# Eight gate projections moved ahead of the attention as four pairs of quarter products, and the softmax multiply moved from VectorE to GpSimd

## The chip, the cores and the metric

The kernel runs on one core of one Trainium2 chip. Five engines of that core run side by side, each in the order of its own instructions: TensorE (PE, with its weight loads PEld), VectorE (DVE), ScalarE (ACT), GpSimd (POOL) and SyncE (SP), which here issues nearly all DMAs. The metric is device time in microseconds, the median of several runs. A trace of one execution is there beside it.

## What is computed

One step of an encoder layer for 1,024 prompt tokens and 64 sample tokens (T = 1,088), model width 1,024. A normalised input is projected to 6,144 columns. Two attention branches of eight heads by 64 follow, and two gates of 1,024 columns each:

```python
h = rms_norm(x, norm_w) @ w_in                       # (1088, 1024) @ (1024, 6144)
sb_q, sb_k, sb_v, sb_z, cb_q, cb_k, cb_v, cb_z, g_sb, g_cb = jnp.split(h, SPLIT_POINTS, axis=-1)
...
# branch A, stick-breaking: beta = sigmoid(q.k/8), w[t,s] = beta[t,s] * prod_{s<j<t} (1 - beta[t,j])
# branch B, band attention: softmax(q.k/8 + rel_bias) over a band of at most 9 chunks of 64 keys
...
b_sb = (o_sb * silu(z_sb)) @ w_proj_sb
b_cb = (o_cb * silu(z_cb)) @ w_proj_cb
h = sigmoid(g_sb) * b_sb + sigmoid(g_cb) * b_cb
y = x + h @ w_out
```

New keys and values are outputs too. Everything is float32; the projections are made of three products each of a high and a low part in a reduced format (high by high, high by low, low by high).

## The kernel before

The order of every engine's instructions is the order of the program (`manual_schedule`, line 38). The stages are:

1. **Natural products** (line 464): eight blocks of 256 columns of the projection, tokens on the partitions.
2. **Pairs** (lines 606 to 657): eight *pairs* of 128-column blocks, listed in `pairs` (lines 145 to 149). A pair is a 2 by 2 product of halves (two halves of the 1,024 inputs, two blocks of columns, two halves of the tokens), made from seven quarter products and sums of them instead of eight. Each quarter product has 24 matmuls: two stretches of tokens `XC` (256 and 288), four blocks of 128 inputs, three parts. `prep` and `presum` make the weights of a quarter product (ACT, POOL, and DVE for the sums) five products ahead; `emit` (line 565) evicts a finished quarter. For a `silu` pair it takes a Sigmoid on ACT and a multiply on DVE, and for a kind `sig`, which is in the code but in no pair before, the Sigmoid alone; the result goes to DRAM.
3. **Attention** (lines 1169 to 1202): 144 steps `seq`, 72 of the stick-breaking branch `sb` and then 72 of the band branch `cb`. A step is one block of query tokens of one head. For each of four head pairs p the blocks come in the order t = 8 (the 64 sample tokens, 576 keys), 0, 1, ... 7, two heads each. In a step with `sb` there are n = 128 (t + 1) keys, with `cb` at most 640.
4. **Merge and output**: projections of the branches (lines 873 and 917) and the last product (line 1404).

In one turn i of the attention's loop the program issues, in this order: `qk(i)`, the scores; half of the turn's filling; `av`, the product with the values, if one is due; `tr(i - 3)`, the transposes of the finished weights of three steps before; `mid(i)`; the other half of the filling.

`qk` multiplies into a buffer `z` of PSUM (three buffers; a step of more than 512 keys takes two). For `sb`, ACT then takes two Sigmoids, into `kp` and `be`. For `cb`, DVE adds the bias and finds the extreme (line 1030), and ACT takes Exp with the sum of the row (line 1034). `mid` is on DVE: for `sb` a scan (line 1044) and a multiply (line 1045), for `cb` the reciprocal of the sum (line 1047) and the multiply of the row by it (line 1048). `tr` transposes on PE into one of two buffers `pt`, and ACT or DVE in turn copies them to `wT` (lines 1085 and 1087). `av` multiplies `wT` by the values, and DVE multiplies the result by the gate `zt` (line 1118). `be` has four buffers, `wT` four.

**The filling.** `run_fill` (line 766) is a generator that gives one matmul at a time: first the `units` (lines 150 and 151), 128 columns of the projection each, 72 matmuls over all tokens in chunks `CH` of 384, 384 and 320, and then the projection of branch `sb`, `proj_sb`, 288 matmuls. Before the change there are 16 units: eight Sigmoid gates of `sb` and eight raw gates of `cb`. The weights of the next unit are split in the second chunk of each unit: the high part on ACT (line 115), the low part on POOL (line 122). Two units (six times `fill(24)`, line 1157) run ahead of step 0; the steps get as many matmuls as lines 1161 to 1188 share out, in proportion to n for `sb` and to n + 150 for `cb`; what is left runs after the loop. Before the last unit the generator stops until the flag `late["sb"]` is set (lines 982 and 1190), in the sixth step of `cb`: what a turn asks for until then is kept in `owed` and asked for at once afterwards.

The attention's inputs come by DMAs that `prefetch` (line 1123) issues on SP. `load_bias` (line 1146) loads a head's bias and has POOL put two masks into it (lines 1150 and 1151), which wait for the load.

Of the kernel before, what the change touches and what calls it, by code (L numbers as in the profile page):

```python
# [10 lines left out]
AF = mybir.ActivationFunctionType  # L11
OP = mybir.AluOpType
# [5 lines left out]
KT = 8  # L18
# [14 lines left out]
def hybrid_step_kernel(ctx: ExitStack, tc: tile.TileContext, x_prompt, x_sample, c_sbk, c_sbv, c_cbk, c_cbv,  # L33
# [3 lines left out]
    V, A, G, TE, SP = nc.vector, nc.scalar, nc.gpsimd, nc.tensor, nc.sync  # L37
# [15 lines left out]
    def rows(t):  # L53
        return 128 if t < 8 else NS
# [26 lines left out]
    d_g = {b: [dram.tile([128, T], F32, name=f"d_g{b}{u}") for u in range(KT)] for b in ("sb", "cb")}  # L81
# [63 lines left out]
    pairs = []  # L145
    for p in (0, 2):
        pairs += [("k", 512 + 128 * p, p), ("q", 128 * p, p)]
    for p in (0, 2):
        pairs += [("silu", 1536 + 128 * p, d_z["sb"][p:p + 2]), ("silu", 3584 + 128 * p, d_z["cb"][p:p + 2])]
    units = [("ev_act", 4096 + 128 * j, (AF.Sigmoid, d_g["sb"][j])) for j in range(KT)]  # L150
    units += [("ev_act", 5120 + 128 * j, (AF.Copy, d_g["cb"][j])) for j in range(KT)]

    def put_t(dst, src):
        A.activation(dst[0], src, AF.Copy)
# [43 lines left out]
    with ExitStack() as ph:  # L198
# [251 lines left out]
        for i in range(nb):  # L450
            for ti, t in enumerate(TO):
                r = rows(t)
# [91 lines left out]
    with ExitStack() as ph:  # L544
# [70 lines left out]
        for i in range(len(pairs)):  # L615
            bank, s1, u2, u3 = {}, {}, {}, {}
            for s in range(7):
                n = 7 * i + s
# [375 lines left out]
    def band(b, t):  # L994
        if t == 8:
            return 0, 576
        if b == "sb":
            return 0, (t + 1) * 128
        k0 = max(0, t - 4)
        return k0, (t + 1 - k0) * 128  # L1000
# [36 lines left out]
    def mid(i):  # L1037
        b, p, t, hd = seq[i]
        r = rows(t)
        k0, n = band(b, t)  # L1040
        be, kp = st[i]
        if b == "sb":
            im = imp[0:64, 960 - n:960] if t == 8 else imp[:, NP - n:NP]
            V.tensor_tensor_scan(kp[:r, n - 1::-1], kp[:r, n - 1::-1], im[:, ::-1], 0.0, op0=OP.mult, op1=OP.add)  # L1044
            V.tensor_tensor(out=be[:r, :n], in0=be[:r, :n], in1=kp[:r, 1:n + 1], op=OP.mult)  # L1045
        else:
            V.reciprocal(kp[:r, 3:4], kp[:r, 2:3])
            V.tensor_scalar(be[:r, :n], be[:r, :n], kp[:r, 3:4], None, op0=OP.mult)

    def wbase(b, j):  # L1050
        return max(0, 2 * j - 4) if b == "cb" and j < 4 else 0
# [106 lines left out]
        flush()  # L1158
        f()
    FP = 180  # L1160
    n_sb = 72 * 7
    n_cb = 72 * (len(units) - 9) + FP
    wt = {"sb": lambda n: n, "cb": lambda n: n + 150}
    tot = {b: sum(wt[b](band(b, t)[1]) for bb, p, t, hd in seq if bb == b) for b in ("sb", "cb")}
    amount = {"sb": n_sb, "cb": n_cb}
# [3 lines left out]
    for i in range(len(seq) + LAG + 1):  # L1169
        m = 0  # L1170
        if i < len(seq):
            b, p, t, hd = seq[i]
# [22 lines left out]
        if 0 <= i - LAG < len(seq):  # L1195
            tr(i - LAG)
            b, p, t, hd = seq[i - LAG]
            if hd == 1 and (t % 2 == 1 or t == 8):
                avq.append((b, p, t // 2 if t < 8 else 4))
        if i < len(seq):  # L1200
            mid(i)
# [175 lines left out]
    for i in range(2):  # L1377
# [3 lines left out]
        for q, s in enumerate(OP_):  # L1381
            n = 8 * i + q
# [13 lines left out]
            for c in range(2) if s != "b" else ():  # L1396
# [9 lines left out]
                p = ps[:]  # L1406
# [17 lines left out]
                if s in (3, 4, 5, 6):  # L1424
# [4 lines left out]
                    if s == 4:  # L1429
                        p, x = u3[c], xrs.pop((i, 1, 1, c))  # L1430
                    V.tensor_tensor(out=y, in0=p, in1=x, op=OP.add)
                    store_y(i, w, half, c, y)
            for s_, wh, wl in ([] if n == 0 else [(0,) + first, (3, wh, wl)] if n == 1 else
                               [(s, wh, wl)] if s in (0, 3, "b", 5) else []):
                w = 0 if s_ in (0, 3) else 1
                r = 0 if s_ in (0, "b") else 1
# [55 lines left out]
```

## Time and profile before

| | |
|---|---|
| median of 3 runs | 1012.59 us (1009.52 to 1013.1) |
| the profiled execution's own time | 1008.24 us |
| its span, first to last instruction | 1006.3 us |
| TensorE's mean granted clock in it | 0.997 |
| busy: PE, DVE, ACT, POOL | 97%, 65%, 47%, 32% |

The profile's page sums each engine's busy time, the chain of work that ended last, and groups of instructions (line, engine, operation, tiles, shape, count, busy time, mean duration, idle time ahead of them and what ended it). Views of the trace cut this by a window of time, by line, by tile, or give the instructions in order. Matmuls overlap in their pipeline, so that the duration of one is longer than the time from one to the next; what a matmul costs is read from a run of them. In the profiled execution the pairs begin at 226.2 us, the first unit at 403.4, the first step of `cb` waits for its bias until 630.9, and the last steps of the attention end at about 855 us.

### The profile page before, as it was taken

Reading aid. Unit: us, or ns where it says so; the run is one execution under the profiler, and the core shown is the slowest. Engines: PE = TensorE matmul, PEld = TensorE weight load, DVE = VectorE, ACT = ScalarE, POOL = GpSimd, SP = SyncE. Lnnn points to the kernel's source line nnn. Section 1 sums busy time; section 2 is a strip of 40 time slices with the busy share of each in tenths; the row PEclk is TensorE's granted clock in tenths of the full one; section 3 lists DMA queues with packets and bytes.
Section 4 is the critical chain, followed back from the end, with each engine's and each line's share of the span. In section 5 each row is a group of like instructions: output and inputs, shape, how many; then the busy total and the mean of one; then the engine's idle time right before and its main releaser. Section 6 shows DMA issues by size and latency. Waiting matters only on the chain.

```text
span 1006.3 us, 20170 instructions
## 1 busy us (share of the span) xinstructions
PE 978.0 (97%) x7512; PEld 929.9 (92%) x7512; DVE 655.2 (65%) x1233; ACT 473.1 (47%) x1075; POOL 322.0 (32%) x338
## 2 busy tenths in 40 slices
PE   5999999999999999999999999999999899989998
PEld 5999999999889999988898878898989798989998
DVE  5466673894354554189798878465766766399735
ACT  5544443444343433277666656454445543366220
POOL 3276663205343543211111101110202200387452
PEclk9999999999999999999999999999999999999999
DMA  6736577434555332697565644775756954863632
GB/s 227 231 105 211 184 247 275 129 100 155 173 163 165 119 98 77 173 244 192 137 169 149 160 116 119 206 201 152 192 151 184 266 168 130 250 213 100 194 128 95
DMA packets 180865, 169.83 MB, mean 169 GB/s; under 512 B 34912, under 2 KB 167136, under 8 KB 180640
## 3 DMA queue, kind: packets, MB, share of 16 engines
q1 hardware_dynamic: 172048, 160.23, 53.7%
q10 hardware_dynamic: 8720, 8.33, 2.6%
q8 instruction: 59, 0.97, 0.4%
q14 instruction: 38, 0.31, 0.1%
HBM read 109.78 MB, written 58.72 MB: 167 GB/s over the span
## 4 chain that ended last, share of the span: by engine, by line
PE 86%; DMA 4%; DVE 3%; ACT 3%; issue 2%; SPq 1%; POOL 1%; DVEq 0%; ACTq 0%
PE acc L464 19%; PE acc L773 17%; PE b L634 15%; PE b L1404 8%; PE o L1115 7%; PE pt L1076 6%; PE b L917 4%; PE z L1025 3%; PE z L1024 3%; PE acc L873 3%; DMA d_ksbT<-hl 1%; PE pk L349 1%; DMA wrawx<-in_w_in_dram 1%; PE pt L277 1%; DVE be L1045 1%
## 5 line engine op out<-in xcount | busy, mean ns | idle before, releaser
L122 POOL TENSOR_TENSOR wlo<-wraw,whi 128x1024 fp32r<-128x1024 f32 x30 | 74.2, 2472 | 245.0 <-ACT whi L115 211.4
L773 PE MATMUL acc<-xm,whi 128*128 128x384 f32 (+1 forms) x384 | 128.6, 335 | 0.0
L1044 DVE TENSOR_TENSOR_SCAN kp<-kp,imp 64x576 f32<-64x576 f32 (+8 forms) x72 | 102.8, 1428 | 21.2 <-ACT kp L1027 21.0
L1034 ACT ACTIVATE be<-be,sm 128x640 f32<-128x640 f32 (+5 forms) x72 | 50.8, 705 | 97.0 <-DVE sm L1030 97.0
L1076 PE MATMUL pt<-ident,be 128*128 128x128 f32 (+2 forms) x608 | 89.5, 271 | 6.2 <-DVE wT L1087 3.4
L1085 ACT ACTIVATE wT<-pt 128x512 f32<-128x512 f32 (+3 forms) x130 | 63.5, 502 | 55.3 <-PE pt L1076 55.3
L1076 PEld LDWEIGHTS pt<-ident,be 128*128 128x128 f32 (+2 forms) x608 | 68.1, 139 | 18.1 <-issue 6.4
L464 PE MATMUL acc<-whi,xa 128*128 128x256 f32 x256 | 74.2, 292 | 0.0
L773 PEld LDWEIGHTS acc<-xm,whi 128*128 128x128 f32 x384 | 72.5, 189 | 1.1
L464 PE MATMUL acc<-wlox,xm 128*128 128x256 f32 x256 | 70.8, 278 | 0.0
L464 PE MATMUL acc<-whi,xm 128*128 128x256 f32 x256 | 70.7, 278 | 0.0
L464 PE MATMUL acc<-wlo,xa 128*128 128x256 f32 x256 | 70.7, 278 | 0.0
L464 PE MATMUL acc<-whix,xb 128*128 128x256 f32 x256 | 70.6, 278 | 0.0
L464 PE MATMUL acc<-whix,xm 128*128 128x256 f32 x256 | 70.6, 278 | 0.0
L1115 PE MATMUL o<-wT,vp 128*64 128x256 f32 (+1 forms) x608 | 67.2, 361 | 0.1
L1045 DVE TENSOR_TENSOR be<-be,kp 64x576 f32<-64x576 f32 (+8 forms) x72 | 60.3, 837 | 10.3 <-DVE kp L1044 0.5
L1027 ACT ACTIVATE kp<-z 128x384 f32<-128x384 f32 (+6 forms) x112 | 54.3, 484 | 24.3 <-PE z L1025 22.9
L773 PE MATMUL acc<-xa,wlo 128*128 128x384 f32 (+1 forms) x192 | 65.4, 341 | 0.0
L773 PE MATMUL acc<-xa,whi 128*128 128x384 f32 (+1 forms) x192 | 65.4, 341 | 0.0
L773 PE MATMUL acc<-xm,wlo 128*128 128x384 f32 (+1 forms) x192 | 65.1, 339 | 0.0
L1115 PEld LDWEIGHTS o<-wT,vp 128*64 128x64 f32 x608 | 43.1, 138 | 23.7 <-issue 8.2
L773 PE MATMUL acc<-xb,whi 128*128 128x384 f32 (+1 forms) x192 | 64.1, 334 | 0.0
(298 smaller groups left out, 3012.6 us busy)
## 6 DMA issues: line engine op xcount, KB each, us to landing
wraw<-in_w_in_dram SPq DMA_DIRECT2D x35, 512.0 KB, 4.5
wrawx<-in_w_in_dram SPq DMA_DIRECT2D x13, 512.0 KB, 4.4
sq<-d_qsbT SPq DMA_DIRECT2D x32, 192.0 KB, 4.8
sq<-d_qcbT SPq DMA_DIRECT2D x32, 192.0 KB, 3.7
gt<-d_gsb SPq DMA_DIRECT2D x30, 192.0 KB, 2.7
xt<-in_x_prompt_dram SPq DMA_DIRECT2D x8, 512.0 KB, 5.7
d_kcbT<-hl SPq DMA_DIRECT2D x8, 512.0 KB, 4.6
d_qcbT<-hl SPq DMA_DIRECT2D x8, 512.0 KB, 5.7
```

Of the source, the lines that this page charges most:

```text
L122: (eng or G).tensor_tensor(out=l, in0=raw, in1=h[:].bitcast(F32), op=OP.subtract)
L464: TE.matmul(ps, x, w, start=m == 0, stop=m == len(steps) - 1)
L634: TE.matmul(ps[:, :m], w[:, hl_, k], right[s](x)[:, k, a:b], start=s < 3 and k == 0 and e == 0, stop=k == 3 and e == 2, skip_group_check=s ...
L773: TE.matmul(ps[:, :b - a], w[:, k], xk(x, k)[:, a:b], start=k == 0 and n == 0, stop=k == KT - 1 and n == 2)
L1027: A.activation(kp[:r, x:y], z[:r, :m], AF.Sigmoid, scale=-0.125)
L1034: A.activation(be[:r, :n], be[:r, :n], AF.Exp, bias=kp[:r, j:j + 1], scale=-1.0, accum_out=kp[:r, 2:3])
L1044: V.tensor_tensor_scan(kp[:r, n - 1::-1], kp[:r, n - 1::-1], im[:, ::-1], 0.0, op0=OP.mult, op1=OP.add)
L1045: V.tensor_tensor(out=be[:r, :n], in0=be[:r, :n], in1=kp[:r, 1:n + 1], op=OP.mult)
L1076: TE.transpose(pt[:kr, x, :r], be[:r, kb * 128:kb * 128 + kr], ident[:r, :r])
L1085: A.activation(w[:, sl:sl + m, q0:q0 + r], pt[:, :m, :r], AF.Copy)
L1115: TE.matmul(o[hd * 64:hd * 64 + 64, c0:c1], vv[:kr, kb, hd * 64:hd * 64 + 64], wT[b, p, j, hd, s // 4][:kr, s % 4, c0:c1], start=si == 0, ...
L1404: TE.matmul(ps[:, t], left[s](xs_, k)[:, ts_], wt_[:, k], start=s < 3 and t == k == e == 0, stop=k == 3 and e == 2, skip_group_check=s > 2 ...
```

## The change

The eight Sigmoid gates of `sb` leave the units and become four pairs of kind `sig` at the end of the list. Eight units, the raw gates of `cb`, stay as filling. The sharing of the filling follows: `sb` gets 360 matmuls of it in place of 504, `cb` 252 in place of 684. The first two units still run ahead of step 0. And in the band attention the multiply by the reciprocal goes from DVE to POOL; the reciprocal stays on DVE.

```diff
@@ -147,8 +147,8 @@
     for p in (0, 2):
         pairs += [("silu", 1536 + 128 * p, d_z["sb"][p:p + 2]), ("silu", 3584 + 128 * p, d_z["cb"][p:p + 2])]
-    units = [("ev_act", 4096 + 128 * j, (AF.Sigmoid, d_g["sb"][j])) for j in range(KT)]
-    units += [("ev_act", 5120 + 128 * j, (AF.Copy, d_g["cb"][j])) for j in range(KT)]
+    pairs += [("sig", 4096 + 128 * p, d_g["sb"][p:p + 2]) for p in range(0, KT, 2)]
+    units = [("ev_act", 5120 + 128 * j, (AF.Copy, d_g["cb"][j])) for j in range(KT)]
 
@@ -1045,7 +1045,7 @@
         else:
             V.reciprocal(kp[:r, 3:4], kp[:r, 2:3])
-            V.tensor_scalar(be[:r, :n], be[:r, :n], kp[:r, 3:4], None, op0=OP.mult)
+            G.tensor_scalar(be[:r, :n], be[:r, :n], kp[:r, 3:4], None, op0=OP.mult)
 
@@ -1158,8 +1158,8 @@
     FP = 180
-    n_sb = 72 * 7
-    n_cb = 72 * (len(units) - 9) + FP
+    n_sb = 72 * (len(units) - 3)
+    n_cb = 72 + FP
     wt = {"sb": lambda n: n, "cb": lambda n: n + 150}
```

## The prediction

> **What bounds the kernel now.** I read the page first, its busy shares and the chain that ended last; then the windows, one for each stage the change touches; then, inside the stages, the groups by line and single stretches in order of time.
>
> ```profile
> span 1006.3 us, 20170 instructions
> PE 978.0 (97%) x7512; PEld 929.9 (92%) x7512; DVE 655.2 (65%) x1233; ACT 473.1 (47%) x1075; POOL 322.0 (32%) x338
> PE 86%; DMA 4%; DVE 3%; ACT 3%; issue 2%; SPq 1%; POOL 1%; DVEq 0%; ACTq 0%
> ```
>
> The chain is TensorE's for 86%. But 65% for DVE is a mean over stages. The windows (columns: length, then PE, PEld, DVE, ACT, POOL busy, granted clock, DMA share, GB/s) are the last pairs, the `sb` steps and the `cb` steps:
>
> ```profile
> 302.20:403.40 101.20, 101.20 (x817) 101.20 (x816) 51.57 (x103) 36.95 (x80) 44.78 (x31) 1.00 0.38 116
> 427.40:630.90 203.50, 199.87 (x1433) 177.45 (x1432) 173.89 (x187) 137.93 (x336) 24.36 (x76) 0.99 0.62 162
> 630.90:846.00 215.10, 212.19 (x1537) 192.84 (x1537) 142.33 (x457) 101.07 (x246) 32.54 (x32) 1.00 0.66 186
> ```
>
> In the pairs nothing but PE matters: it is busy for 101.20 of 101.20 us and DVE for half. In `sb` PE is still full, but DVE is busy for 173.9 of 203.5 us, 85%. So work taken off PE there is worth its full length only for the first 29.6 us, and less where DVE's work doesn't lie evenly.
>
> **What PE gains.** The pairs' line, first and seventh quarter product (count, minimum/median/maximum ns, first and last start), and from the chain a run of the first two units and two runs of the product with the values:
>
> ```profile
> L634 PE MATMUL b<-xa,whi x128: 276/290/369, 226.2 to 385.4; 128*128 128x256 f32 x64, 128*128 128x288 f32 x64
> L634 PE MATMUL b<-xm,wlo x128: 277/290/365, 245.5 to 403.3; 128*128 128x256 f32 x64, 128*128 128x288 f32 x64
> ```
>
> ```profile
> 403.60 23.73 PE acc L773 x144
> 639.53 3.39 PE o L1115 x32
> 845.41 2.31 PE o L1115 x24
> ```
>
> In the last pair the first product's last matmul starts at 385.4 and the seventh's at 403.3: six products in 17.9 us, 2.98 each, 20.9 a pair. Four pairs add **83.5 us**. A unit's 72 matmuls take 23.73/2 = 11.9 us (0.165 a matmul, 0.454 ns a column), so eight units take away **94.9 us**. The difference, 11.4 us, is the seven products in place of eight, and all that PE can gain. The added pairs need a Sigmoid but not the multiply of the `silu` pairs, whose stage already leaves DVE, ACT and POOL half idle; their preparations, weight loads and stores go on at the same pace beside a DMA share of 0.38. The eight weight loads of 512 KB and the stores of the gates leave SP's queue in the attention for SP's queue in the pairs, where the `silu` pairs store as much. I add nothing for all this; if that cover failed, each late block would show as idle PE ahead of L634.
>
> Of the units' 576 matmuls, 144 (23.7 us) leave the `sb` steps and 432 (71.2 us) the `cb` steps: 504 to 360 and 684 to 252. With the 144 ahead of the steps, 756 are shared out, eight units and 180 of `proj_sb` as before, so nothing more is left for the end. The two stages would fall to 179.8 and 143.9 us if PE stayed the bound. The question is how much of it they give back.
>
> **`sb`.** DVE's 173.9 us against 179.8: 97%. (Five splits of unit weights run there in place of seven, so DVE is blocked a little less by POOL.) What an even share hides shows where the small steps (t = 8, 0, 1) follow the large ones:
>
> ```profile
> 477.83 0.66 PE L1076 MATMUL pt<-ident,be 128*128 128x128 f32 x4 [0.59 <-DVE wT L1087]
> 573.47 0.93 PE L1076 MATMUL pt<-ident,be 128*128 128x128 f32 x7
> 580.27 1.15 PE L1076 MATMUL pt<-ident,be 128*128 128x128 f32 x8 [2.40 <-DVE wT L1087]
> 582.42 4.52 PE L1115 MATMUL o<-wT,vp 128*64 128x256 f32 x32
> 582.00:583.00 1.00, 1.00 (x6) 0.48 (x7) 0.87 (x3) 0.50 (x3) 0.10 (x1) 0.50 0.00 0
> ```
>
> Here PE stood for 2.40 us: the `pt` buffer it wanted was to be emptied by a DVE copy, queued behind scans and multiplies. Right behind it the granted clock is 0.50, and the product with the values takes 4.52 us, against 3.39 for the same 32 matmuls in the chain. Such a place costs some 3.5 us. It happened in full once in the three changes of head pair inside `sb` (0.59 us of it in another, the first row), with 7 filling matmuls a step at t = 8; now there are 5, and 9 in place of 12 in the steps at t = 7. I expect it nearly each time: bounds 0 and 12 us, I take **5**, nearer to the row's once than to all three.
>
> The Trainium skill (TensorE: Matmul & The Clock Gate, Part 1) gives the half clock after about 3.4 us without work. Here 2.4 us were enough, and the row decides; by the page's figure these places would cost about 1.1 us less each.
>
> **`cb`.** The reciprocal waits for the sum of Exp, Exp waits for the bias step, and the next bias step stands behind the reciprocal on DVE: a loop through DVE and ACT, whatever PE does. Its groups, and the multiply that leaves it:
>
> ```profile
> L1030 DVE CUSTOM_DVE_ANT_0 be<-z,bias 128x320 f32<-128x320 f32 (+5 forms) x72 | 34.6, 481 | 9.6 <-PE z L1025 5.9 <-DMA bias<-d_rb 2.8 <-DMA d_gcb<-sg 0.3
> L1030 DVE CUSTOM_DVE_ANT_0 be<-z,bias,sm 128x320 f32<-128x320 f32 (+1 forms) x40 | 21.7, 543 | 5.8
> L1030 DVE DVE_READ_ACCUMULATOR2_ANT sm<- 128x1 f32 (+1 forms) x112 | 9.1, 81 | 0.0
> L1034 ACT ACTIVATE be<-be,sm 128x640 f32<-128x640 f32 (+5 forms) x72 | 50.8, 705 | 97.0 <-DVE sm L1030 97.0
> L1034 ACT ACTIVATION_READ_ACCUMULATOR be<-be,sm 128x1 f32 (+1 forms) x72 | 13.4, 187 | 0.0
> L1047 DVE RECIPROCAL sm<-sm 128x1 f32<-128x1 f32 (+1 forms) x72 | 11.4, 158 | 17.2 <-ACT be L1034 16.7
> L1048 DVE TENSOR_SCALAR be<-be,sm 128x640 f32<-128x640 f32 (+5 forms) x72 | 43.5, 605 | 2.5
> ```
>
> ```profile
> 713.79 0.48 DVE L1030 CUSTOM_DVE_ANT_0 be<-z,bias 128x320 f32<-128x320 f32 x1
> 714.43 0.55 DVE L1030 CUSTOM_DVE_ANT_0 be<-z,bias,sm 128x320 f32<-128x320 f32 x1
> ...
> 716.04 0.17 DVE L1047 RECIPROCAL sm<-sm 128x1 f32<-128x1 f32 x1 [1.05 <-ACT be L1034]
> 716.24 0.56 DVE L1048 TENSOR_SCALAR be<-be,sm 128x640 f32<-128x640 f32 x1
> 716.71 0.48 DVE L1030 CUSTOM_DVE_ANT_0 be<-z,bias 128x320 f32<-128x320 f32 x1
> ```
>
> The loop is 34.6 + 21.7 + 9.1 + 50.8 + 13.4 + 11.4 = 141.0 us for 72 steps; with the multiply 184.5, below the present 215 but above 143.9. So the move to POOL is needed: without it the stage could not go below 184.5, and the change would cost some 30 us more. With it the loop (141) and PE (144) are equal, which isn't free. At n = 640 a turn of the loop is 716.21 - 713.79 = 2.42 us. PE needs 0.58 for the scores (1280 columns), 0.65 for five transposes (seven took 0.93 at 573.47, 0.13 each), and 0.71 for 4.3 filling matmuls (252 x 790/46,128 by the sharing rule): 1.94; in every fourth step 2.31 more for the values. Four steps: PE 10.1, loop 9.7, step by step the larger one 11.5. The three `z` buffers, two to a step, let PE be 1.5 steps ahead at most, so part of the 14% is paid: on 144 us, 0 to 20. I take **7**, since before the loop with its multiply was at 184.5 of 215 and the stage lost little.
>
> **The change from `sb` to `cb`.** The sequence that PE fills now: `cb`'s first bias loads, their time to landing (minimum/median/maximum), and the filling matmuls in the first five steps:
>
> ```profile
> 631.00 0.45 DVE L1030 CUSTOM_DVE_ANT_0 be<-z,bias 64x288 f32<-64x288 f32 x1 [2.77 <-DMA bias<-d_rb]
> DMA to landing us min/median/max: 2.6/5.0/6.9
> 626.00:645.40 19.40, 12.19 (x60) 9.84 (x59) 1.00 0.68 183
> ```
>
> 60 filling matmuls, 9.9 us, cover the wait. After the change seven units are done exactly when `sb` ends (144 + 360 = 504), the generator stands before its last unit, and these five steps get none. Their share, about 37 matmuls (6.1 us), comes at once in the sixth. The wait for the bias and the loops of t = 8 remain. Bounds 0 and 10 (the 6.1 us, and a halved clock behind the gap); I take **5**.
>
> **POOL.** 72 multiplies, and what stands in its queue:
>
> ```profile
> L434 POOL TENSOR_TENSOR wlo<-ws,wlo 128x512 fp32r<-128x512 f32 x16 | 21.7, 1358 | 15.2 <-ACT wlo L433 10.1 <-PE acc L464 4.9
> L248 POOL TENSOR_SCALAR rsn<-msn 128x4 f32<-128x4 f32 x32 | 9.1, 284 | 25.9 <-DVE msn L321 25.3
> L122 POOL TENSOR_TENSOR wlo<-wraw,whi 128x1024 fp32r<-128x1024 f32 x30 | 74.2, 2472 | 245.0 <-ACT whi L115 211.4 <-DMA vs<-d_cbv 13.4 <-PE pt L1076 8.4
> ```
>
> No row has a wide one-input operation of POOL. From below 0.28 us (4 columns), from above 1.7 (1.358 x 640/512, two inputs); I take 1.2, nearer to the row of like width. The mean width is 491, so 72 cost some 66 us of about 160. The multiply waits for DVE's reciprocal; queued behind it on POOL are the next masks, splits and low parts (L839), and the transposes wait for it. From scores to transposes are three steps, 7.5 us at n = 640; 0.6 + 2.42 + 1.2 = 4.2 leaves 3.3 of cover. A split (2.47) fits in it. But POOL's masks wait for the bias, 5.0 us from issue, and the multiplies of t = 4 stand behind them: 6.9 us would be about 1.4 late, three times, and a split met in the short steps 1.7. Bounds 0 and 9; I take **1**.
>
> The Trainium skill (GPSIMD Engine Reference, 4.1 Engine selection) advises VectorE for elementwise work, but puts one-input operations near line rate; an estimate from 3.1's 1.03 cycles an element is 0.55 us, and by it this term is 0.
>
> **Sum.** 83.5 - 94.9 + 5 + 7 + 5 + 1 = +6.6 us: 1014.8 against the profiled execution's 1008.24 (span 1006.3). That execution lay 4.35 below the median of the runs, so on 1012.59 I say **1019**.
>
> **Rivals.** *PE stays the bound* (faster): the buffers smooth the loop, and only some 6 us are given back: -5.4, 1007. It decides if less than 6.3 us come back; 0.5%, 5.1 us, is about what a measurement here can tell from no change. For it: before, both stages ran within 4 us of PE's busy time. Against it: 85% then, 97% now. Chance 0.25. *Break-even*: 6.3 to 16.5 us come back, about 1012; 0.28. *My forecast*, the loop and DVE take over: 0.35. *POOL's queue is late* at masks and splits: 8 us more, 1027; 0.12. *The change doesn't share as it says*, with filling left for the end: the count of 756 excludes it.
>
> So faster 0.25, same 0.28, slower 0.47. With nothing given back it is 1001, with every upper bound 1052; 8 in 10 I put at 1004 to 1032, which takes in the POOL case and most of the fast one.
>
> **What would show it.** Right: the `sb` window near 185 us with DVE above 90%; `cb` near 157, bias steps following reciprocals without a gap; PE idle before L1076 at changes of head pair, with a clock below 1; no L773 in `cb`'s first five steps. Wrong: PE busy through both stages (the fast rival), transposes waiting for POOL (its queue), idle PE in the added pairs.

## The result, and the profile after

The change makes the kernel slower: median 1048.01 us of 4 runs (1044.45 to 1052.26) against 1011.06 of 4 runs of the kernel before (1007.77 to 1013.1), a ratio of 1.037, 95% interval 1.032 to 1.0421. The forecast was 1019, with a range to 1032: the direction was right and the size was not. The profiled execution took 1044.45 us, 36.2 more than the one before; the account below is made between these two.

The page's first lines and the shares of its chain:

```profile
span 1042.7 us, 20691 instructions
...
PE 984.6 (94%) x7608; PEld 926.7 (89%) x7608; DVE 639.2 (61%) x1217; ACT 486.9 (47%) x1111; POOL 451.3 (43%) x430
...
PE 71%; DVE 10%; DMA 5%; SPq 4%; ACT 4%; issue 3%; POOL 2%; DVEq 0%; ACTq 0%; POOLq 0%
```

TensorE's busy time rose by only 6.6 us, and its share of the chain fell from 86% to 71%. So 29.8 of the 36.4 us by which the span grew are time in which PE stands. The windows of the stages say where (columns as before the change):

```profile
301.30:486.00 184.70, 184.70 (x1489) 184.70 (x1488) 81.46 (x161) 68.35 (x149) 83.47 (x59) 1.00 0.37 112
510.00:699.00 189.00, 173.85 (x1270) 149.78 (x1268) 170.59 (x187) 132.97 (x328) 21.36 (x74) 1.00 0.60 160
699.00:882.60 183.60, 161.70 (x1129) 134.64 (x1131) 101.73 (x385) 88.75 (x221) 123.53 (x97) 0.95 0.68 185
```

| stage | before, us | after, us | difference | forecast |
|---|---|---|---|---|
| start to end of the pairs | 403.4 | 486.0 | +82.6 | +83.5 |
| two units ahead of the steps | 24.0 | 24.0 | 0 | 0 |
| `sb` steps | 203.5 | 189.0 | -14.5 | -18.7 |
| `cb` steps | 215.1 | 183.6 | -31.5 | -58.2 |
| after the steps | 160.3 | 160.1 | -0.2 | 0 |

In the pairs PE is busy for the whole 184.70 us, with a clock of 1.00. In `sb` it stands for 15 us, in `cb` for 22, and there the clock of 0.95 adds to it. The `cb` steps are 26.7 us longer than forecast, and that is nearly the whole miss.

Three things are to be seen in the `cb` steps. First, the loop through DVE and ACT, in order of time on DVE at n = 640:

```profile
779.30 0.16 DVE L1047 RECIPROCAL sm<-sm 128x1 f32<-128x1 f32 x1 [0.58 <-ACT be L1034]
779.42 0.49 DVE L1030 CUSTOM_DVE_ANT_0 be<-z,bias 128x320 f32<-128x320 f32 x1
779.84 0.08 DVE L1030 DVE_READ_ACCUMULATOR2_ANT sm<- 128x1 f32 x1
780.07 0.55 DVE L1030 CUSTOM_DVE_ANT_0 be<-z,bias,sm 128x320 f32<-128x320 f32 x1
...
781.67 0.17 DVE L1047 RECIPROCAL sm<-sm 128x1 f32<-128x1 f32 x1 [0.58 <-ACT be L1034]
781.79 0.49 DVE L1030 CUSTOM_DVE_ANT_0 be<-z,bias 128x320 f32<-128x320 f32 x1
```

The bias step comes right behind the reciprocal, and DVE has stood 0.58 us for Exp ahead of it. The step takes 781.79 - 779.42 = 2.37 us, and so it does, within 0.03 us, in 20 of the 31 steps of t = 4 to 7: there the loop sets the step. Before, most of these steps took 2.85 to 3.6.

Second, POOL's multiplies by shape (count, then busy us and mean ns):

```profile
L1048 POOL TENSOR_SCALAR be<-be,sm 128x640 f32<-128x640 f32 x32 | 60.4, 1898 | 9.9 <-DVE sm L1047 9.7
...
L1048 POOL TENSOR_SCALAR be<-be,sm 128x128 f32<-128x128 f32 x8 | 5.0, 622 | 10.1 <-DVE sm L1047 8.6 <-DVE sm L1030 1.5
```

1.90 us at 640 columns, where 1.2 was taken and 1.7 was the upper bound; (1898 - 622)/512 = 2.49 ns a column. Third, PE's and POOL's waits in the stage (total us, times, longest), and one place of them in time, on SP, POOL and PE:

```profile
PE pt L1076 <- POOL be L1048: 12.4, 6, 7.3
PE z L1024 <- DVE sm L1030: 7.1, 6, 4.9
```

```profile
POOL bias L1150 <- DMA bias<-d_rb: 32.9, 6, 13.7
```

```profile
726.49 3.20 SPq L51 DMA_DIRECT2D kss<-d_ccbT  x4
729.74 2.51 SPq L51 DMA_DIRECT2D kss<-d_kcbT  x4
...
734.40 2.08 SPq L1149 DMA_DIRECT2D bias<-d_rb  x2
```

```profile
738.60 0.14 POOL L1150 MEMSET bias<- 64x64 f32 x1 [9.87 <-DMA bias<-d_rb]
...
741.02 5.60 POOL L1048 TENSOR_SCALAR be<-be,sm 128x640 f32<-128x640 f32 x3
```

```profile
742.96 1.33 PE L1076 MATMUL pt<-ident,be 128*128 128x128 f32 x5 [7.26 <-POOL be L1048]
...
744.61 0.47 PE L1024 MATMUL z<-ks,sq 128*128 128x320 f32 x1
```

The next heads' bias loads are issued by SP only at 734.40, behind eight loads that take it 5.7 us to issue. SP was late before that: until 721.02 it had stood for POOL, which was to free a buffer with a low part (L839), and from then on it issues nearly without a stop:

```profile
SPq L830 <- POOL xb L839: 6.1, 1, 6.1
```

POOL has come to the mask long before and stands 9.87 us (the longest wait of the view, 13.7, is for the first bias of the stage, where no multiply stands behind it); the multiplies of three steps have piled up behind it; PE stands 7.26 us for the first of them, and then the same matmul of 320 columns takes 0.47 us in place of 0.31: the granted clock is 0.50 from 740.5 to 747.2. That step, t = 5 of the first head pair, took 11.02 us, the same step of the second pair 6.61.

### The profile page after: what moved, and what is told of

Same layout as the page of the kernel before. It is cut to its first block, busy times and chain, and to the rows that moved or that the text cites. A ratio compares the mean times of both kernels' runs of the same rounds, so it can differ in the third digit from the quotient of the medians.

```text
span 1042.7 us, 20691 instructions
## 1 busy us (share of the span) xinstructions
PE 984.6 (94%) x7608; PEld 926.7 (89%) x7608; DVE 639.2 (61%) x1217; ACT 486.9 (47%) x1111; POOL 451.3 (43%) x430
## 4 chain that ended last, share of the span: by engine, by line
PE 71%; DVE 10%; DMA 5%; SPq 4%; ACT 4%; issue 3%; POOL 2%; DVEq 0%; ACTq 0%; POOLq 0%
PE b L634 22%; PE acc L464 18%; PE b L1404 7%; PE o L1115 6%; DVE kp L1044 4%; PE pt L1076 4%; PE b L917 3%; PE acc L773 3%; DVE be L1045 2%; SPq L51 2%; DVE be L1030 2%; PE z L1025 1%; ACT be L1034 1%; PE z L1024 1%; PE acc L873 1%
## 5 line engine op out<-in xcount | busy, mean ns | idle before, releaser
L1048 POOL TENSOR_SCALAR be<-be,sm 128x640 f32<-128x640 f32 (+5 forms) x72 | 108.8, 1518 | 34.6 <-DVE sm L1047 31.8
L1076 PE MATMUL pt<-ident,be 128*128 128x128 f32 (+2 forms) x608 | 95.8, 280 | 26.1 <-POOL be L1048 12.4
L1044 DVE TENSOR_TENSOR_SCAN kp<-kp,imp 64x576 f32<-64x576 f32 (+8 forms) x72 | 98.7, 1371 | 21.4 <-ACT kp L1027 21.4
L122 POOL TENSOR_TENSOR wlo<-wraw,whi 128x1024 fp32r<-128x1024 f32 x22 | 56.4, 2564 | 88.2 <-ACT whi L115 81.1
L1115 PE MATMUL o<-wT,vp 128*64 128x256 f32 (+1 forms) x608 | 74.7, 358 | 5.0 <-DVE wT L1087 2.6
L1115 PEld LDWEIGHTS o<-wT,vp 128*64 128x64 f32 x608 | 46.0, 137 | 32.2 <-DVE wT L1087 6.2
L1024 PE MATMUL z<-ks,sq 128*128 128x320 f32 (+4 forms) x192 | 63.6, 334 | 2.3 <-DVE sm L1030 2.3
L773 PE MATMUL acc<-xm,whi 128*128 128x384 f32 (+1 forms) x192 | 65.3, 340 | 0.0
L1025 PE MATMUL z<-ks,sq 128*128 128x320 f32 (+4 forms) x192 | 63.1, 331 | 0.0
L1015 POOL MEMSET kp<- 128x1 f32 (+1 forms) x72 | 6.6, 98 | 128.6 <-DVE be L1045 128.6
L1027 ACT ACTIVATE kp<-z 128x384 f32<-128x384 f32 (+6 forms) x112 | 55.1, 492 | 13.9 <-PE z L1025 11.7
L642 DVE TENSOR_TENSOR u<-b,s 128x256 f32<-128x256 f32 (+1 forms) x48 | 21.0, 441 | 62.4 <-PE b L634 61.7
```

Source lines behind the costliest of these rows:

```text
L773: TE.matmul(ps[:, :b - a], w[:, k], xk(x, k)[:, a:b], start=k == 0 and n == 0, stop=k == KT - 1 and n == 2)
L1024: TE.matmul(z[:r, :m], s[:, 2 * hd, q0:q0 + r], ks[:, hd, o + x:o + y], start=True, stop=False)
L1025: TE.matmul(z[:r, :m], s[:, 2 * hd + 1, q0:q0 + r], ks[:, hd, o + x:o + y], start=False, stop=True)
L1048: G.tensor_scalar(be[:r, :n], be[:r, :n], kp[:r, 3:4], None, op0=OP.mult)
L1076: TE.transpose(pt[:kr, x, :r], be[:r, kb * 128:kb * 128 + kr], ident[:r, :r])
L1115: TE.matmul(o[hd * 64:hd * 64 + 64, c0:c1], vv[:kr, kb, hd * 64:hd * 64 + 64], wT[b, p, j, hd, s // 4][:kr, s % 4, c0:c1], start=si == 0, ...
```

## The experiments

Two theories stood at first. **L**: the loop sets the `cb` steps, since two engines that are each busy for some 140 us and hand over step by step cost the larger of the two in each step; the masks and the change of stage add a little. **Q**: POOL's queue sets them, since its multiply is slower than thought. Where a single execution is given, its kernel before ran beside it: 1007.6 us beside the first four below, 1009.34 beside the later masks alone and the earlier flag alone, 1008.38 beside the other four. The four runs of the kernel after lie 7.8 us apart, and the start of the `cb` steps differs by up to 8 us between executions of nearly the same kernel. So a few us in the time of a single execution mean little, and stages are compared, from the first bias step of `cb` to the last (182.4 us in the kernel after).

**The multiply back on DVE** (the kernel after):

```diff
-            G.tensor_scalar(be[:r, :n], be[:r, :n], kp[:r, 3:4], None, op0=OP.mult)
+            V.tensor_scalar(be[:r, :n], be[:r, :n], kp[:r, 3:4], None, op0=OP.mult)
```

> The changed kernel with the multiply of the cb steps back on DVE. Theory L (in cb the loop of bias step, Exp and reciprocal through DVE and ACT sets the step, 2.37 us at n = 640): the multiply lengthens every turn by its 0.5 to 0.6 us, a step at n = 640 takes 2.9 us, the cb stage grows from 184 us to about 200, the whole to about 1062 us; the waits of PE for POOL go. Theory Q (the queue of POOL, 1.9 us a multiply, sets the stage): the stage shrinks to 175 or less, the whole to 1036 or less.

```profile
702.20:897.60 195.40, 165.63 (x1125) 132.13 (x1127) 133.07 (x454) 88.33 (x221) 18.48 (x26) 0.97 0.63 172
```

1060.14 us. The stage is 13.0 us longer, and most steps at n = 640 take 2.85 to 2.92 us. POOL is nearly out of the stage (18.48 us), and it is slower still: POOL's queue is not what sets it. The loop grew by the multiply's 0.56 us, and so did the step.

**The multiply on POOL in the kernel before** (the same line, the other way):

> The kernel before with the multiply on POOL and nothing else changed. L: PE's filling (3.0 us a step at n = 640) is above the loop either way, so within 6 us of before, some of the masks' delay included. Q: the multiplies come late here too, 10 us or more above before.

```profile
632.20:850.40 218.20, 211.54 (x1523) 191.14 (x1522) 103.87 (x383) 101.85 (x245) 135.48 (x102) 0.99 0.66 183
```

1013.38 us, 5.8 more than the kernel before beside it. DVE's 38 us less in the stage win nothing where PE is busy for 211.54 of 218.20 us. The stage even became 4.4 us longer (213.8 before). All of it lies in the third head pair, 62.5 us against 58.3; why stays open.

**The multiply left out** (the kernel after without line 1048):

```diff
-            G.tensor_scalar(be[:r, :n], be[:r, :n], kp[:r, 3:4], None, op0=OP.mult)
```

> The changed kernel without the multiply by the reciprocal (the band attention's rows stay unnormalised); the reciprocal stays. L: only the waits of PE for POOL go (some 11 us in two places of the cb stage), the step at n = 640 stays at 2.37 us, the whole is near 1034 us. Q: the stage falls to PE's need, about 150 us, the whole to about 1010.

1039.45 us; the stage falls from 182.4 to 168.1, and most steps at n = 640 stay at 2.25 to 2.37. So POOL in all its ways is worth 14.3 us, and the loop without any multiply still sets the step. Neither theory has the stage alone.

**The reciprocal a step later.** In the kernel after, `mid` of a `cb` step is issued behind the scores of the next one, so that the bias step no longer stands behind a reciprocal that waits for Exp:

```diff
             qk(i)
+            if i and seq[i - 1][0] == "cb":
+                mid(i - 1)
...
-        if i < len(seq):
+        if i < len(seq) and seq[i][0] == "sb":
             mid(i)
```

> The changed kernel with the reciprocal and the POOL multiply of a cb step issued one step later, behind the next step's bias step on DVE, so that no bias step waits for the Exp before it. L: the step at n = 640 falls below 2.37 us, the stage from 184 to 160 or 165, the whole to about 1022 us. Q: the multiplies come a step later still, the stage is as long or longer, 1043 or more.

DVE in order of time at n = 640:

```profile
782.07 0.49 DVE L1030 CUSTOM_DVE_ANT_0 be<-z,bias 128x320 f32<-128x320 f32 x1
...
783.19 0.16 DVE L1047 RECIPROCAL sm<-sm 128x1 f32<-128x1 f32 x1
783.27 0.67 DVE L1087 COPY wT<-pt 128x512 f32<-128x512 f32 x1
783.86 0.48 DVE L1030 CUSTOM_DVE_ANT_0 be<-z,bias 128x320 f32<-128x320 f32 x1
```

The reciprocal no longer waits, and most undisturbed steps fall from 2.37 to between 1.65 and 2.0 us, about PE's 1.94. But the stage came to 168.3 us and the time to 1036.03, since the masks are still there: the step at t = 5 of the first head pair takes 14.46 us. Over the stage they cost 11.3 us here, as the run with both, below, shows (168.3 to 157.0).

**The same with the multiply on DVE** (line 1048 as in the first experiment):

> e4 with the multiply back on DVE, both it and the reciprocal one step late. If the loop was the whole reason against DVE: the cb stage is set by DVE's own work (142 us before) and PE's need (144), about 160 us without the masks' waits for POOL, the whole near 1028, below e4's 1036. If DVE's added 43 us still bind: a step at n = 640 near 2.4 us, the whole at 1040 or more.

1031.94 us, stage 164.2: below the version on POOL, though not as low as expected, and 31.2 below the stage with the multiply in the loop. Once the loop is broken, DVE is no bad place for the multiply; with the masks as they are, it came out 4.1 us of stage better than POOL, each measured once.

**The bias earlier, its masks later** (the kernel after; the loads at t = 1 in place of 4, the two masks apart from them at t = 5):

```diff
-        if b == "cb" and t == 4:
+        if b == "cb" and t == 1:
             load_bias(2 * np_)
             load_bias(2 * np_ + 1)
+        if b == "cb" and t == 5:
+            mask_bias(2 * np_)
+            mask_bias(2 * np_ + 1)
```

> The changed kernel with one edit: the next bias loads at t = 1, their masks at t = 5. The two steps that stood behind the masks (11.0 and 6.6 us) fall to about 3.4, the cb stage from 184 to about 173 us, the whole to about 1034.

```profile
700.00:868.60 168.60, 157.37 (x1121) 130.49 (x1121) 99.82 (x382) 88.14 (x221) 122.52 (x96) 0.98 0.74 201
```

1033.92 us. The stage falls by 13.8 us, PE's wait for POOL's multiplies from 12.4 us to 1.3, the steps at t = 5 from 11.02 and 6.61 us to 2.64 and 2.74, and the clock rises from 0.95 to 0.98. POOL's multiplies are as long as before: it is the wait in its queue, not the multiply, that cost. The stage without any multiply, 168.1, is no more than 0.5 us shorter than this one. The first head pair takes 49.5 us here (58.5 in the kernel after), the second, undisturbed, 40.5.

**Both**, the diffs of the later reciprocal and of the later masks, the multiply on POOL:

> e4 with the next bias loads issued at t = 1 in place of t = 4 and their masks put in at t = 5, so that POOL's multiplies don't stand behind masks that wait for a load. If the two long steps of e4 (t = 5, second head: 14.5 and 4.9 us against 3.7 in the last head pair) come from that wait: both fall to about 4, the whole from 1036 to about 1024 us. If they come from the late DMAs themselves or from proj_sb's start: no change beyond 2 us.

```profile
703.40:860.40 157.00, 148.83 (x1117) 127.97 (x1118) 96.22 (x381) 88.23 (x219) 120.47 (x96) 0.98 0.78 214
```

1024.18 us, stage 157.0, as low as the forecast had thought of the change as it is. Against the run with the later masks alone (168.6) it is the loop by itself that is broken here: 11.6 us.

**The flag earlier.** In the kernel after, the filling's last unit is released in the first step of `cb` and not in the sixth:

```diff
-        if i < len(seq) and seq[i][:3] == ("cb", 0, 1) and hd == 1:
+        if i < len(seq) and seq[i][:3] == ("cb", 0, 8) and hd == 0:
```

> The changed kernel with one edit: the flag for the last unit set in the first cb step in place of the sixth. If the filling held back costs its own length (37 matmuls, 6.1 us): the 8.4 us step at t = 1 falls to about 2 us, the first head pair of cb, 58.5 us, to about 53. If the gap at the change of stage is DVE's and the bias load's: the filling only moves, the head pair is shorter by 2 us or less.

1039.95 us. The first head pair falls from 58.5 to 51.4 us: its sixth step, in which all that was held back came at once, from 8.37 to 1.84. Part of the filling moves into the steps ahead of it, so that the first six fall by 4.5 us together (21.1 to 16.6); most of the rest is the step at the masks, 8.95 in place of 11.02.

**All copies of `sb` on ACT** (the kernel after; DVE had every fourth):

```diff
-                if flip[0] % 2 or b == "sb" and flip[0] % 4:
+                if flip[0] % 2 or b == "sb":
```

> The changed kernel with all wT copies of the sb steps on ACT (DVE had a quarter of them). If DVE's queue sets the sb stage (busy 171 us, 10 us of gaps between scan and multiply, 189 us of stage): DVE has 11 us less to do and PE no longer waits for its copies, the stage falls by 8 to 12 us, the whole to about 1036. If PE or ACT set it: within 3 us of the changed kernel.

```profile
512.40:690.50 178.10, 170.07 (x1261) 148.19 (x1259) 161.68 (x164) 137.59 (x348) 20.58 (x75) 1.00 0.64 169
```

1032.46 us. From its first scan to the first bias step, `sb` falls from 187.7 to 178.1 us. ACT takes 24 copies, and gets busier without harm; DVE's queue set the stage.

**All of these together**, the diffs of "both" and of the copies, and the flag with the second step:

```diff
-        if i < len(seq) and seq[i][:3] == ("cb", 0, 1) and hd == 1:
+        if i < len(seq) and seq[i][:3] == ("cb", 0, 8) and hd == 1:
```

> e5 and e6 together, and the flag for the last unit set in the second cb step in place of the sixth, so that the filling isn't held back. If each of the places found is a loss of its own: 1036 less 12 (masks) less 9 (sb copies) less 4 (filling held back), about 1011 us, level with before. If the filling held back costs nothing: 1015.

```profile
690.60:845.40 154.80, 149.50 (x1117) 129.43 (x1118) 94.34 (x379) 88.39 (x221) 120.89 (x96) 0.98 0.80 217
```

1009.68 us against 1008.38: with everything repaired, the change is where it started.

**Further**, three more edits on the kernel of the run before: the low parts of five units' weights on DVE in place of POOL, the first two heads' bias in buffers of their own and loaded during the last head pair of `sb`, the flag in the first step.

```diff
-                            W.split(("u", j + 1) if j + 1 < len(units) else ("p", 0))
+                            W.split(("u", j + 1) if j + 1 < len(units) else ("p", 0), V if 1 < j + 1 < 7 else None)
...
-        if b == "cb" and t == 4:
+        if (b == "cb" or nb_ == "cb") and t == 1:
...
-        bt = late["y"].tile([128, 640], F32, name="bias", bufs=4)
+        bt = (am if h < 2 else late["y"]).tile([128, 640], F32, name="bias0" if h < 2 else "bias", bufs=2 if h < 2 else 4)
```

> e7 with three more repairs: the low parts of the unit weights that are split in the sb steps on DVE (on POOL each held DVE up by 1.9 us, five times); the first two heads' bias loaded at t = 1 of the last sb head pair into buffers of their own, and masked at t = 5 (in e7 DVE waited 3.1 us for it and PE 6.3 us behind it); the flag set in the first cb step. DVE needs about 1.1 us for a low part, so 4 us there, and 4 to 6 us at the change of stage: about 1001 us, 0.993 of before. If PE's other work simply moves into these gaps: no change against e7, 1009.

**The kernel before with the same repairs**, its eight gates still units, its multiply on DVE and its flag as it was; it has the diffs of the later reciprocal, the later masks, the copies and the first heads' bias, and of the low parts this one:

```diff
-                            W.split(("u", j + 1) if j + 1 < len(units) else ("p", 0))
+                            W.split(("u", j + 1) if j + 1 < len(units) else ("p", 0), V if 1 < j + 1 < 9 else None)
```

> The kernel before (gates as filling, multiply on DVE) with the same repairs as e9_more, the flag apart: late reciprocal and multiply, masks out of the way, sb copies on ACT, low parts in sb on DVE, early first bias. If the stages there are PE's, the repairs can only win the 4.5 us and 3.6 us in which PE stood: 1002 to 1006 us. If the repairs, not the change, are what e9_more gains by, the two are equal; if the change's 11.4 us of PE work come through, e9_more is below this one by 5 us or more.

The two ran on the same chip, beside 11 runs of the kernel before (median 1010.04). The first has a median of 1002.67 us of 6 (1001.55 to 1007.0), ratio 0.9923, interval 0.9898 to 0.9948. The second has 1003.04 of 6 (999.34 to 1003.21), ratio 0.9916, interval 0.9893 to 0.9939. Both beat the kernel before by some 0.8%, and neither the other: the repairs gain some 7 us, the change nothing. Their two stages, first with the change and then without it:

```profile
516.10:693.30 177.20, 175.20 (x1275) 153.05 (x1274) 158.97 (x168) 137.48 (x348) 9.96 (x74) 0.98 0.66 175
693.30:843.80 150.50, 145.03 (x1106) 124.54 (x1105) 94.33 (x381) 88.40 (x221) 120.39 (x92) 1.00 0.80 215
```

```profile
432.00:625.70 193.70, 192.96 (x1406) 171.73 (x1405) 161.59 (x170) 143.37 (x356) 9.70 (x74) 1.00 0.67 175
625.70:840.20 214.50, 212.62 (x1545) 193.53 (x1544) 137.40 (x450) 102.45 (x247) 31.86 (x28) 1.00 0.65 181
```

The stages differ by 16.5 and 64.0 us, 80.5 of the 94.9 that the units take; the pairs cost 82.6. With the change PE stands for 2.0 and 5.5 us in them, without it for 0.7 and 1.9, which makes 4.9. In `sb` with the change the clock was 0.50 for 6.7 us, an estimated 3.4 us of full clock lost; that execution was also the longest of its six. The rest of the 14.4, some 6, stays open.

## Why the prediction was wrong in size

**Right: what PE gains.** Four pairs cost 82.6 us (83.5 forecast) with PE never idle; the filling was shared out to the end, and the tail is unchanged. (The 756 leaves out 24 filling matmuls that line 1186 adds at the change of stage, before as after.) That the units, once gone, free their full 94.9 us is not shown: with the repairs in both kernels it was 80.5.

**Right: the multiply must leave the loop.** With it on DVE the stage was 195.4 us, above the 184.5 that the loop's groups add up to. But it was 13.0 us longer than with POOL, not some 30, since the stage with POOL was itself far above 144.

**Wrong in size: `sb`, 5 forecast, 9.2 measured** (189.0 - 179.8), within the bounds. The failed step is "DVE's 173.9 us against 179.8: 97%". It took DVE's busy time for the time that DVE is occupied. The groups of DVE in the stage, before and after, have idle time ahead of the multiply behind each scan, nearly none of it ended by another engine:

```profile
L1045 DVE TENSOR_TENSOR be<-be,kp 64x576 f32<-64x576 f32 (+8 forms) x72 | 60.3, 837 | 10.3 <-DVE kp L1044 0.5 <-PE z L1025 0.5
```

```profile
L1045 DVE TENSOR_TENSOR be<-be,kp 64x576 f32<-64x576 f32 (+8 forms) x72 | 62.2, 863 | 9.6
```

9.6 us over 72 steps are 0.13 each, between a scan and the multiply that needs its result. After the change 170.6 + 9.6 = 180.2 us are DVE's own, and DVE waits for other engines only 4.4 us. PE's 179.8 is too long in turn. From the first scores of `sb` to the first of `cb` the kernel before takes 198.8 us, and with the repairs 193.2, with the same matmuls on PE: so PE, busy as it looked, was already being held up. Less 23.7 that leaves PE 169.5 us; the kernel after takes 183.3, and with the copies on ACT 172.3. DVE is the longer engine, and what it holds up is what was given back.

The place that the forecast priced, a halved clock behind a stand at the change of head pair, was not it. PE stood up to 2.03 us behind DVE's copies, and the clock in the window is 1.00 all the same. That it stayed so is chance, as the last section shows.

**Wrong in size: the loop of `cb`, 7 forecast, 11.6 measured by its edit and about 17 by difference**, within the bounds. The failed step is "so part of the 14% is paid ... I take 7". The stage is 183.6 - 143.9 = 39.7 us above PE's share; the masks are 13.8 of it (the run with later masks), the first head pair beyond an undisturbed one 9.0 (49.5 - 40.5), and the rest is 16.9. Of this the later reciprocal takes away 11.6, once the masks are out of its way; the other 5.3 are not shown to be the loop's. Some 3.6 of them are filling that did not leave: 22 of the 60 matmuls that covered the wait before had run ahead of the first bias step, and so in the window of `sb`. The four steps' arithmetic had much of the answer in it, "step by step the larger one 11.5": three steps at the loop's 2.37 and a fourth at PE's 1.94 + 2.31 are 11.4, and the last four of the second head pair, 2.39, 2.37, 2.75 and 3.73, took 11.2. There the buffers smooth out almost nothing. In the four steps before, t = 4 and 5, the product with the values has 16 matmuls in place of 24, an estimated 1.5 us; the same sum is 10.6, and in the run with later masks these steps took 9.8 to 10.3, so that part of it was smoothed. The argument for 7, that the stage lost little before with a loop of 184.5, compared two different cases. The window of the second head pair before:

```profile
686.20:739.00 52.80, 52.80 (x391) 48.09 (x390) 34.26 (x111) 24.20 (x60) 5.48 (x6) 1.00 0.63 170
```

PE is busy in all of it, and the steps at n = 640 take 2.85 to 2.92 us or more. By the forecast's own rates PE, with 11.7 filling matmuls, needed 0.58 + 0.65 + 1.93 = 3.16 us in such a step, and the loop with its multiply 2.91 (the first experiment): the larger one step by step was PE itself. After the change the larger one is the loop in three steps and PE in the fourth, and where that one has 24 matmuls for the values both are paid. The run with the later reciprocal breaks the loop, and the steps fall to PE's.

**Wrong in size: POOL, 1 forecast, 13.8 measured**, outside the bounds of 0 and 9. Two steps failed. The multiply's duration was 1.90 us, above the bound from the row of 512 columns with two inputs; its own price in time is small, since PE's wait for it is 1.3 us in the run with later masks, and that stage is only 0.5 us longer than the one without any multiply. The one that counts is "POOL's masks wait for the bias, 5.0 us from issue". It counted from the issue as if this came with POOL's turn; but SP had stood 6.1 us for POOL, issues the bias behind eight other loads, at 0.63 to 0.80 us each (2.51/4 and 3.20/4), and POOL stood 9.87 us for it in the first head pair and 6.05 in the second. The forecast named the wait, POOL's queue and those behind it, and didn't look at the queue in which the load itself stands. Added to it is the half clock behind PE's gap.

**Wrong in size: the change of stage, 5 forecast, about 9 measured**, within the bounds of 0 and 10. The mechanism was as told: no filling in the first five steps and a lump in the sixth. The 9 is the first head pair's excess over the second in the run with later masks. The run with the earlier flag takes 4.5 us away in the first six steps, and 2.6 behind them; the wait for the first bias stays.

**The sum.** 82.6 - 94.9 + 9.2 + 39.7 - 0.2 = +36.4, the growth of the span (36.2 in the times). Each of the four terms came out above its forecast, by some two thirds or more. "Every upper bound" was 1052, and 1048 is close to it.

**The rivals.** PE stays the bound: refuted in both stages. Break-even, with at most 16.5 us given back: 48.7 came back. POOL's queue late at the masks: it happened, and at 13.8 us it cost more than the 8 of that rival, on top of the loop.

## What to carry to other kernels

Filling matmuls hide loops, queues and waits for loads; before moving them away, set beside what is left of TensorE the occupied time of every other engine, with the gaps between its own dependent instructions, and where two come out equal, take the larger one step by step. Before giving an engine's queue a step that others wait for, follow every foreign wait in that queue back to the issue of what it waits for. Where a result goes round through two in-order engines, try asking for it one step later than it could be: here that was worth 11.6 us.

## What the runs showed of the hardware

A multiply by a value per partition costs POOL 622 ns at 128 columns and 1898 at 640, 2.49 ns a column. The Trainium skill (GPSIMD Engine Reference, 4.1 Engine selection) puts one-input operations near line rate; for this operation the rows do not agree.

A weight split on POOL holds up DVE's two-input operations. In the kernel after, two multiplies of the same shape on DVE, and the split beside the first of them on POOL:

```profile
524.35 2.60 DVE L1045 TENSOR_TENSOR be<-be,kp 128x512 f32<-128x512 f32 x1
...
528.54 0.69 DVE L1045 TENSOR_TENSOR be<-be,kp 128x512 f32<-128x512 f32 x1
```

```profile
523.77 2.62 POOL L122 TENSOR_TENSOR wlo<-wraw,whi 128x1024 fp32r<-128x1024 f32 x1 [3.85 <-ACT whi L115]
```

The first takes 1.9 us longer, and ends 0.56 us after the split. The Trainium skill (SBUF — State Buffer, Who interferes with whom) says that a VectorE instruction with two SBUF inputs contends with a GpSimd instruction that reads SBUF, and the rows agree. DVE's bias step, one of whose inputs is in PSUM, is hardly slower beside POOL's multiplies (491 ns at 320 columns, 484 before).

Whether the granted clock halves behind a stand of PE of some 2 us differs between executions. Ahead of the same transposes of `sb` PE stood 2.03 us in the kernel after and 2.04 in the run without the multiply of `cb`; behind it the clock (third number from the end) was 1.00 in the one and 0.50 in the other:

```profile
638.20 0.87 PE L1076 MATMUL pt<-ident,be 128*128 128x128 f32 x6 [2.03 <-DVE wT L1087]
638.20:641.60 3.40, 3.40 (x21) 3.01 (x23) 3.27 (x3) 2.03 (x5) 0.09 (x1) 1.00 0.95 232
```

```profile
644.58 1.53 PE L1075 MATMUL pt<-ident,be 128*128 128x128 f32 x6 [2.04 <-DVE wT L1086]
644.70:648.00 3.30, 3.30 (x13) 3.20 (x14) 3.17 (x3) 0.87 (x2) 0.09 (x1) 0.50 0.98 200
```

In the repaired kernel with the change even a stand of 0.95 us is followed by 6.7 us at 0.50 (520.90 to 527.60).
